# Folding a pooling mixer's product into the output weights, and a re-ordered start of the kernel

## The chip, the cores and the metric

The kernel runs on one core of a Trainium2 chip. The metric is the device time of one execution in microseconds (us), lower is better. The engines are TensorE (PE in the profile, its weight loads PEld), VectorE (DVE), ScalarE (ACT), GpSimd (POOL) and SyncE (SP), which issues nearly all transfers between DRAM and on-chip memory.

## The reference

One transformer-like layer (DEPTH = 1) is computed in fp32 for a prompt of 2048 tokens and a sample of 64, D = 1024, four heads of 128, feed-forward width 2816:

```
mod = c_act @ w_ada + b_ada                        # adaLN shifts, scales, gates
h   = rmsnorm(x) * g1 * (1 + scale1) + shift1
u, q, k, v, o, gates = split(h @ w_in)
diff = pooled(u) - u                               # 4 groups of 128, windows 2, 4, 8, 16
y    = einsum('btgc,gcd->btgd', diff, w_pool) * s_pool
x   += gate1 * (concat(y, mlstm(q, k, v, o, gates)) @ w_out)
x   += gate2 * (conv_gated(norm(x) @ w_up) @ w_down)
out  = rmsnorm(x) * g_final
```

The pooling mixer's y is thus a linear function of `diff`: for group gi, y @ w_out[rows of gi] is diff @ (w_pool[gi] * s_pool) @ w_out[rows of gi].

## The kernel before

**Arithmetic.** Each fp32 operand of a large product is split into two fp32r halves, hi (a rounded copy) and lo (the remainder), and a product is three fp32r matmuls (hi hi, hi lo, lo hi). A weight block is split by `work_out`: ScalarE writes hi (L345), VectorE writes lo (L348). Small steps (row sums with ones, transposes, gate columns, the heads' 128 x 128 products) are plain fp32; such a matmul leaves two records in the profile.

**Stages.** Four groups of tokens (512, 512, 512, 576) go through the attention part one after the other: v's projection (`proj_v`, L1018; for group 0 `first`, L949), four heads (`proj_qko`, with `gemm` L411, and `lstm`, whose fp32 steps are L1158 to L1246), four pooling inputs (`gemm`) each followed by `poolmix` (L1302), then `outproj` (`gemm`, L574 adds the residual). Three groups of 704 tokens go through the feed-forward part (L1444 and L1698), which the change leaves alone.

**The pooling product.** `poolmix` forms diff, splits it, multiplies it by the split w_pool (`WPO`, three matmuls at L1302 for each block of tokens), and writes the scaled result as two halves again (ScalarE L1304, VectorE L1305), which `outproj` multiplies by w_out's rows.

**Weights.** `issue` starts the load of the next block of the list `stream`; `pump` keeps up to seven split blocks (WB) and four raw ones (RB) on the way. In group 0 a block's split halves are stored in DRAM (`hl_kept`, by `keep`, L353), and groups 1 to 3 load these (512 KB, for v 528 KB) instead of a raw block (256 or 264 KB).

**The start.** `first` loads x, then the adaLN weights for shift1 and scale1 in four quarters (`load_q`, `mod_q`: products L864, transpose L870), and for each quarter makes two of h's eight row blocks (`h0`: L888, L889, L893) and their v products (`cells`). It needs the reciprocal norms in every partition, which TensorE makes by ones (`pr`, L929).

**Order.** The start up to v's projection of group 0 is in hand-written order. In the rest of the attention part a scheduler orders each engine's instructions by its own estimates; the program gives it side work in generators that are ticked at set places: bg[3] is `ada` (the rest of the adaLN modulation: VectorE steps L180 and L182 on streamed w_ada, then sums by ones L190 and transposes L197), others are `rstd_rows` (reciprocal norms, L466 and L473), the next group's norm, the lstm heads. Every engine runs its instructions in order, SyncE its transfers too.

Of the kernel before, what the change touches and what calls it, by code (L numbers as in the profile page):

```python
# [16 lines left out]
P = 128  # L17
# [20 lines left out]
WB, RB = 7, 4  # L38
# [7 lines left out]
NV = 360  # L46

C_ID = 0

C_L127, C_L63, C_CNT = 0, 128, 256  # L50
NCST = 448
# [3 lines left out]
def tile_layer(ctx: ExitStack, tc: tile.TileContext, xT, vecs, cst, rst, rowv, w_mod, w_ada, w_qkou, w_v, w_pool,  # L55
# [51 lines left out]

    live = [0]
# [5 lines left out]
    x0 = [big(mx.tile([P, 2, TMAX], F32R, tag="mx", name=f"mx{k}")) for k in range(KD)]  # L114
    for k in range(KD):
        (act if k % 2 else nc.sync).dma_start(out=x0[k][:, :GT], in_=xT[k, :, 0:GT])
    V = cp.tile([P, NV], F32, tag="V", name="V")
    nc.sync.dma_start(out=V, in_=vecs)
    ident = cp.tile([P, P], F32, tag="ident", name="ident")
    nc.sync.dma_start(out=ident, in_=cst[:, C_ID:C_ID + P])  # L120
    RV = cp.tile([4, 3], F32, tag="RV", name="RV")
    nc.sync.dma_start(out=RV, in_=rowv)
# [26 lines left out]
    def ada(m, first):  # L149
# [36 lines left out]
        yield  # L186
# [6 lines left out]
        yield  # L193
# [11 lines left out]
        yield  # L205
# [29 lines left out]
    U_ORDER = (3, 2, 1, 0)  # L235
    OUT, INSIDE, WHOLE = range(3)
    stream = []

    hl_kept = dr.tile([40, P, 2, WN], F32, tag="hl_kept", name="hl_kept")
# [12 lines left out]
    for g in range(NG):  # L252
        rows = [[halves((hv, kh), w_v[hv][kh], 4 * VC[hv]) for kh in (0, 1)] for hv in (1, 0)]
# [9 lines left out]
        for n in range(KD):  # L263
            stream += [(w_out[n][:, c:c + 512], 512) for c in (512, 0)]
# [196 lines left out]
    def rstd_rows(ssum, o, out):  # L461
# [8 lines left out]
        yield  # L470
# [73 lines left out]
    def stat2(o, ssum):  # L544
        for _ in range(5):
            yield
        out = RS2[:, 4 * o.g:4 * o.g + len(o.chunks)]
        if o.last:
            rstd_cols([ssum], o, out)
        else:  # L550
            yield from rstd_rows(ssum, o, out)
        yield

    def outproj(o, mix, between):
# [28 lines left out]
        bg[0].append(stat2(o, ssum))  # L583
# [193 lines left out]
    if True:  # L777
# [3 lines left out]
        C = a1.tile([P, NCST - P], F32, tag="C", name="C")  # L781
# [31 lines left out]

        def rows_of(o):
# [9 lines left out]
        def norm1(o, xs, box):  # L824
# [8 lines left out]
            yield from rstd_rows(ssum, o, rs)  # L833
            yield
# [7 lines left out]
        spare_rows = [x[:, GT:2 * GT] for x in x0]  # L842
        c_q = [spare_rows,
# [5 lines left out]
        def load_q(qn):  # L849
            for k in range(KD):  # L850
                tc.keep_in_program_order(nc.sync.dma_start(out=c_q[qn][k], in_=w_mod[qn, k]))
# [996 lines left out]
```

## Time and profile before

| what | value |
|---|---|
| median of 3 runs | 2243.78 us (2242.88 to 2245.01) |
| profiled execution | 2241.11 us, its span 2239.3 us |
| TensorE busy | 2215.4 us (99%) |
| VectorE / ScalarE busy | 1568.4 us (70%) / 990.7 us (44%) |
| first product of a head (L411) | at 58.91 us |
| mean granted TensorE clock | 0.995 |
| moved by DMA | 493.71 MB, mean 220 GB/s |

The span runs from the first to the last instruction of the profiled execution. The clock is TensorE's granted one, 1.00 is full speed. A group of instructions has a busy time and a mean duration; since matmuls overlap in the array, the mean of one is longer than the step from one to the next in an unbroken run. "Idle before" is the time that an engine stood still ahead of an instruction, with what ended it. A timeline gives an instruction's start, its duration, and in brackets the idle time ahead of it; a run of equal instructions is one row. The DMA share is the mean busy share of 16 DMA engines.

### The profile page before, as it was taken

Reading aid. Unit: us, or ns where it says so; the run is one execution under the profiler, and the core shown is the slowest. Engines: PE = TensorE matmul, PEld = TensorE weight load, DVE = VectorE, ACT = ScalarE, POOL = GpSimd, SP = SyncE. Lnnn points to the kernel's source line nnn. Section 1 sums busy time; section 2 is a strip of 40 time slices with the busy share of each in tenths; the row PEclk is TensorE's granted clock in tenths of the full one; section 3 lists DMA queues with packets and bytes.
Section 4 is the critical chain, followed back from the end, with each engine's and each line's share of the span. In section 5 each row is a group of like instructions: output and inputs, shape, how many; then the busy total and the mean of one; then the engine's idle time right before and its main releaser. Section 6 shows DMA issues by size and latency. Waiting matters only on the chain. (4 is left out here: it accounts for less than half of the span.)

```text
span 2239.3 us, 37881 instructions
## 1 busy us (share of the span) xinstructions
PE 2215.4 (99%) x13720; PEld 2100.6 (94%) x13720; DVE 1568.4 (70%) x2878; ACT 990.7 (44%) x1968; POOL 209.1 (9%) x482
## 2 busy tenths in 40 slices
PE   8999999999999999999999999999999999999998
PEld 6888888888899999999999999999999999999997
DVE  4878558667855788687858587777666675767474
ACT  3544335234233455465536344545444343435254
POOL 0010000001000230010000210100001210101012
PEclk8999999999999999999999999999999999999999
DMA  9967997997989485657556884566448655353442
GB/s 337 337 244 257 336 300 224 331 314 234 308 286 308 131 268 174 224 174 261 196 177 229 267 272 159 173 202 199 144 160 287 199 170 163 116 172 111 149 144 79
DMA packets 286139, 493.71 MB, mean 220 GB/s; under 512 B 24920, under 2 KB 88920, under 8 KB 285952
## 3 DMA queue, kind: packets, MB, share of 16 engines
q1 hardware_dynamic: 276480, 468.97, 63.5%
q10 hardware_dynamic: 9472, 22.32, 2.6%
q8 instruction: 108, 1.77, 0.3%
q14 instruction: 79, 0.65, 0.1%
HBM read 382.97 MB, written 108.22 MB: 219 GB/s over the span
## 5 line engine op out<-in xcount | busy, mean ns | idle before, releaser
L1444 PE MATMUL mm<-hx,wt 128*128 128x352 f32 x5544 | 898.4, 323 | 2.8 <-DVE wt L348 2.0
L1444 PEld LDWEIGHTS mm<-hx,wt 128*128 128x128 f32 x5544 | 893.1, 188 | 3.7 <-DVE wt L348 2.3
L1698 PE MATMUL mm<-av,wt 128*128 128x352 f32 (+2 forms) x3168 | 514.4, 323 | 0.0
L1698 PEld LDWEIGHTS mm<-av,wt 128*128 128x128 f32 x3168 | 509.0, 188 | 1.6
L411 PE MATMUL mm<-hl,wt 128*128 128x512 f32 (+2 forms) x1920 | 390.6, 358 | 1.2 <-DVE wt L348 0.9
L411 PEld LDWEIGHTS mm<-hl,wt 128*128 128x128 f32 x1920 | 314.2, 188 | 53.2 <-issue 5.3
L348 DVE TENSOR_TENSOR wt<-raw,wt 128x512 fp32r<-128x512 f32 (+3 forms) x494 | 307.1, 637 | 71.3 <-ACT wt L345 68.3
L345 ACT ACTIVATE wt<-raw 128x512 fp32r<-128x512 f32 (+3 forms) x494 | 270.6, 570 | 158.6 <-PE mm L1698 71.1
L1714 DVE SCALAR_TENSOR_TENSOR x<-mm,MOD,x 128x352 f32<-128x352 f32 (+4 forms) x224 | 106.4, 525 | 126.1 <-PE mm L1698 126.0
L411 PE MATMUL mm<-mx,wt 128*128 128x512 f32 (+1 forms) x960 | 187.6, 355 | 0.3 <-DVE scr L574 0.2
L411 PEld LDWEIGHTS mm<-mx,wt 128*128 128x128 f32 x960 | 159.1, 188 | 26.8 <-ACT mx L1304 1.0
L1431 DVE SCALAR_TENSOR_TENSOR tg<-eg,V,tg 128x704 f32<-128x704 f32 (+1 forms) x132 | 125.7, 952 | 53.8 <-ACT tg L1426 51.5
L348 DVE TENSOR_TENSOR wt<-wt 128x512 fp32r<-128x512 f32 x176 | 122.1, 694 | 37.2 <-ACT wt L345 37.0
L1431 DVE SCALAR_TENSOR_TENSOR ta<-ea,V,ta 128x704 f32<-128x704 f32 (+1 forms) x132 | 125.6, 952 | 5.3 <-ACT ta L1426 2.6
L345 ACT ACTIVATE wt<-wt 128x512 fp32r<-128x512 f32 x176 | 108.5, 623 | 25.2 <-DMA wt<-wsum 20.9
L1492 ACT ACTIVATE u<-mm 128x352 f32<-128x352 f32 x66 | 30.6, 464 | 165.4 <-PE mm L1444 161.2
L1452 DVE TENSOR_TENSOR eg<-mm,u 128x352 f32<-128x352 f32 x154 | 70.2, 468 | 42.0 <-ACT u L1507 28.3
L1552 DVE TENSOR_TENSOR av<-tg,av 128x704 fp32r<-128x704 f32 (+1 forms) x88 | 60.5, 708 | 53.1 <-ACT av L1547 53.0
L1538 ACT ACTIVATE tg<-tg 128x704 f32<-128x704 f32 (+1 forms) x66 | 52.4, 794 | 78.7 <-DVE tg L1431 78.7
L1483 ACT ACTIVATE s<-mm 128x352 f32<-128x352 f32 x66 | 30.5, 462 | 102.4 <-PE mm L1444 100.2
L1018 PE MATMUL mm<-wt,hl 128*128 128x256 f32 (+1 forms) x576 | 72.4, 285 | 0.0
L1018 PEld LDWEIGHTS mm<-wt,hl 128*128 128x128 f32 x576 | 70.7, 188 | 1.0 <-issue 0.6
(295 smaller groups left out, 1993.5 us busy)
## 6 DMA issues: line engine op xcount, KB each, us to landing
wt<-hl_kept SPq DMA_DIRECT2D x108, 512.0 KB, 5.8
raw<-w_up SPq DMA_DIRECT2D x198, 256.0 KB, 4.0
wt<-wsum SPq DMA_DIRECT2D x176, 256.0 KB, 4.4
wt<-wsplit SPq DMA_DIRECT2D x88, 512.0 KB, 5.0
raw<-w_down SPq DMA_DIRECT2D x96, 256.0 KB, 3.8
w<-w_up SPq DMA_DIRECT2D x88, 256.0 KB, 4.2
wsum<-w SPq DMA_DIRECT2D x44, 512.0 KB, 4.7
wsplit<-wt SPq DMA_DIRECT2D x44, 512.0 KB, 4.5
```

Of the source, the lines that this page charges most:

```text
L345: act.activation(u.w[:, 0, :u.n], u.raw[:, :u.n], AF.Copy)
L348: dve.tensor_tensor(out=u.w[:, 1, :u.n], in0=u.raw[:, :u.n], in1=u.w[:, 0, :u.n].bitcast(F32), op=ALU.subtract)
L411: pe.matmul(ps[bi][:, :hi - lo], U[:, a, k % 4 * P:(k % 4 + 1) * P], mv[k][:, b, lo:hi], start=(at == 0 and pi == 0), stop=(k == order[-1] ...
L1018: pe.matmul(ps[ti][:n, :cols], h[4 * kh + k4][:, b, lo:lo + n], U[:, a, k4 % 2 * cols:(k4 % 2 + 1) * cols], start=(kh == 0 and k4 == 0 and ...
L1431: dve.scalar_tensor_tensor(out=t[:, :E], in0=ext[:, j:j + E], scalar=wc(j, f), in1=t[:, :E], op0=ALU.mult, op1=ALU.add)
L1444: pe.matmul(ps[:, :FH], U[:, a, kc * P:(kc + 1) * P], Bo.at(nm, kc, b), start=(first and kc == 0 and pi == 0), stop=(kc == 3 and pi == 2), ...
L1452: dve.tensor_tensor(out=ext[:, d:d + b - a], in0=ps[:, a:b], in1=u[:, a:b], op=ALU.add)
L1492: act.activation(self.u2, b1[:, :FH], AF.Copy)
L1538: act.activation(self.tg[:, :E], self.tg[:, :E], AF.Silu)
L1552: dve.tensor_tensor(out=self.d[:, 1, a:b], in0=self.tg[:, a + 2 * s:b + 2 * s], in1=self.d[:, 0, a:b].bitcast(F32), op=ALU.subtract)
L1698: pe.matmul(ps[i][:, :hi - lo], U[:, a, k % 4 * P:(k % 4 + 1) * P], av[k][:, b, lo:hi], start=(k == 0 and (a, b) == PASSES[0]), stop=(k == ...
L1714: dve.scalar_tensor_tensor(out=x3[n][:, a:b], in0=ps[i][:, a - lo:b - lo], scalar=gt2(n, s), in1=x3[n][:, a:b], op0=ALU.mult, op1=ALU.add)
```

## The change

Five things are changed at once.

1. *Fold.* A new generator `fold` multiplies w_out's first 512 columns of each of the eight blocks (all that touches the pooled rows) once by w_pool scaled by s_pool (`WPT`, the transposed w_pool, scaled on ScalarE): 32 plain-fp32 matmuls (L843 of the changed kernel) in eight steps, eight ScalarE copies, four loads and four stores of 512 KB; `outproj` streams the result `wo_in` in place of these columns. `poolmix` ends with the split of diff: L1302, L1304 and L1305 are gone. w_out's pieces are loaded into buffers (`w4`, four of them) that `ada` uses as well.
2. *Queue of fp32 steps.* `fold`, the end of `ada` (`ada_end`) and `rstd_rows` are put into a list `side`; `extra()` runs one step of it, at three places of the gates' work and three of each head, next to fp32 steps that stand there already.
3. *First loads.* x comes in four loads of 512 KB, three of the four adaLN quarters in pairs; the identity and the gate biases lie in `vecs`, without loads of their own.
4. *Start.* `pr` comes after five of the eight blocks of the first adaLN quarter; x is multiplied by `pr` straight from PSUM; two matmuls whose result is not used stand ahead of v's products; of the first quarter the products with hi rows come first; a quarter's adaLN products are one block behind 6, 4 or 4 runs of three v products (PRE), no longer mixed with these.
5. *v.* The split halves of v's weights are not stored; groups 1 to 3 load the raw blocks and split them again (eight blocks a group). RB is 5.

In the order of the built kernel TensorE's start reads as follows (before: L864 adaLN products, L929 `pr`, L870 transpose, L949 v's products; the tile names behind `<-` are the operands). Before:

```order
L864 MATMUL m_183<-mx_90,CA 2x128 x4
L864 MATMUL m_183<-mx_91,CA 2x128 x4
L929 MATMUL pr<-scr,ones_r 128x512
L870 MATMUL m_184<-ident,scr 128x128
L949 MATMUL mm<-wt,hl_306 128x264 x12
L949 MATMUL mm<-wt,hl_307 128x264 x3
L864 MATMUL m_183<-q,CA 2x128 x8
L864 MATMUL m_183<-k,CA 2x128 x8
L949 MATMUL mm<-wt,hl_307 128x264 x3
L864 MATMUL m_183<-th,CA 2x128 x8
L949 MATMUL mm<-wt,hl_307 128x264 x3
L864 MATMUL m_183<-at,CA 2x128 x8
```

With the change (L905 is now the adaLN product, L983 `pr`, L914 the transpose, L996 the unused products, L1014 v's):

```order
L905 MATMUL m_168<-mx_90,CA 2x128 x4
L983 MATMUL pr<-scr,ones_r 128x512
L905 MATMUL m_168<-mx_90,CA 2x128 x4
L905 MATMUL m_168<-mx_91,CA 2x128 x8
L914 MATMUL m_169<-V,scr 128x128
L996 MATMUL pr<-mx_87 128x256 x2
L1014 MATMUL mm<-wt,hl_291 128x264 x8
L1014 MATMUL mm<-wt,hl_292 128x264 x8
L1014 MATMUL mm<-wt,hl_291 128x264 x2
L905 MATMUL m_168<-q,CA 2x128 x8
L905 MATMUL m_168<-k,CA 2x128 x8
L905 MATMUL m_168<-th,CA 2x128 x8
```

`pr` moved ahead of the last 12 adaLN products, and the next quarter's products stand together.

TensorE in group 0's first head, from the transpose of the gates' rows (L1110 before) to the products with the transposed gates `CL` (L1122) and the first 128 x 128 product of keys and queries. Before:

```order
L1110 MATMUL m_911<-ident,R_188 128x128 x4
L411 MATMUL mm<-hl_594,wt 128x512 x3
L411 MATMUL mm<-hl_306,wt 128x512 x3
L411 MATMUL mm<-hl_307,wt 128x512 x3
L1170 MATMUL m_956<-ident,k 128x128 x4
L411 MATMUL mm<-hl_393,wt 128x512 x3
L411 MATMUL mm<-hl_394,wt 128x512
L1122 MATMUL m_929<-CL,C 128x16
L1158 MATMUL m_949<-RHL,E_r 128x512
```

With the change (L1170 is now that transpose, L429 the heads' product, L1183 the product with CL, L843 the fold):

```order
L1170 MATMUL m_892<-V,R_173 128x128 x4
L843 MATMUL m_901<-w_751,WPT 128x128 x4
L429 MATMUL mm<-hl_567,wt 128x512 x3
L1183 MATMUL m_916<-CL,C 128x16
L843 MATMUL m_919<-w_751,WPT 128x128 x4
L429 MATMUL mm<-hl_291,wt 128x512 x3
L429 MATMUL mm<-hl_292,wt 128x512 x3
L1220 MATMUL m_945<-RHL,E_r 128x512
L1232 MATMUL m_952<-V,k 128x128 x4
L1242 MATMUL m_958<-q,k 128x128 x4
L843 MATMUL m_964<-w_926,WPT 128x128 x4
```

Between the transpose and the product with CL stood thirteen matmuls of the heads' product and a transpose of k; now a fold step and three matmuls stand there.

VectorE around v's projection of group 1 (L574 is outproj's residual, L182 an adaLN step on streamed w_ada, L1032 the gates' copy after a v product, L803 a sum of w_up's blocks). Before:

```order
L574 SCALAR_TENSOR_TENSOR scr<-mm,MOD,scr 128x512
L446 TENSOR_TENSOR ssum<-ssum,scr 128x512
L180 TENSOR_SCALAR s_2678<-raw,CA 128x512
L180 TENSOR_SCALAR acc<-raw,CA 128x512
L182 SCALAR_TENSOR_TENSOR s_2678<-raw,CA,s_2678 128x512
L182 SCALAR_TENSOR_TENSOR acc<-raw,CA,acc 128x512
L1032 COPY gt<-mm 128x8
L803 TENSOR_TENSOR w_2312<-w_2312 128x256
```

With the change (L589, L198, L1091 and L821 are these; L366 is the split's lo half):

```order
L589 SCALAR_TENSOR_TENSOR scr<-mm,MOD,scr 128x512
L198 SCALAR_TENSOR_TENSOR s_2541<-raw,CA,s_2541 128x512
L198 SCALAR_TENSOR_TENSOR u<-raw,CA,u 128x512
L464 TENSOR_TENSOR ssum<-ssum,scr 128x512
L198 SCALAR_TENSOR_TENSOR s_2541<-raw,CA,s_2541 128x512
L198 SCALAR_TENSOR_TENSOR u<-raw,CA,u 128x512
L198 SCALAR_TENSOR_TENSOR s_2541<-raw,CA,s_2541 128x512
L366 TENSOR_TENSOR wt<-raw,wt 128x512
L1091 COPY gt<-mm 128x8 x3
L198 SCALAR_TENSOR_TENSOR u<-raw,CA,u 128x512
L1091 COPY gt<-mm 128x8
L366 TENSOR_TENSOR wt<-raw,wt 128x512
```

Two splits of v's blocks now stand among the adaLN steps.

The diff, cut to its core:

```diff
-WB, RB = 7, 4
+WB, RB = 7, 5
+FIRST, PRE = 5, (6, 4, 4)
+    side = []
+    def extra():
+        while side:
+            try:
+                next(side[0])
+                return
+            except StopIteration:
+                side.pop(0)
...
     for g in range(NG):
-        rows = [[halves((hv, kh), w_v[hv][kh], 4 * VC[hv]) for kh in (0, 1)] for hv in (1, 0)]
+        rows = [[[(w_v[hv][kh][:, c:c + 2 * VC[hv]], 2 * VC[hv]) for c in (0, 2 * VC[hv])] for kh in (0, 1)] for hv in (1, 0)]
...
-            stream += [(w_out[n][:, c:c + 512], 512) for c in (512, 0)]
+            stream += [(w_out[n][:, 512:], 512), (wo_in[n], 512)]
...
+        def fold():
+            for n in range(0, KD, 2):
+                w = a1.tile([P, 4, 256], F32, tag="w4", name="w4", bufs=4).rearrange("p (a b) c -> p a (b c)", a=2)
+                nc.sync.dma_start(out=w, in_=w_out[n:n + 2, :, :512].rearrange("n p c -> p n c"))
+                yield
+                for i in range(2):
+                    t = w[:, i]
+                    ps = m2_ps()
+                    for gi in range(4):
+                        c = slice(gi * P, (gi + 1) * P)
+                        pe.matmul(ps[:, c], WPT[:, c], t[:, c], start=True, stop=True)
+                    act.activation(t, ps, AF.Copy)
+                    if i == 0:
+                        yield
+                nc.sync.dma_start(out=wo_in[n:n + 2].rearrange("n p c -> p n c"), in_=w)
...
             mod = mod_q(0)
-            for _ in range(KD):
+            for _ in range(FIRST):
                 next(mod)
-            load_q(3)
...
             pe.matmul(pr, ones, dg[:, :GT], start=True, stop=True)
             act.activation(pb[0], pr, AF.Copy)
+            for k in (0, 1):
+                dve.tensor_tensor(out=x0[k], in0=x0[k], in1=pr, op=ALU.mult)
+            for _ in range(KD - FIRST):
+                next(mod)
+            load_q(3)
...
+            for _ in range(2):
+                pe.matmul(pr[:, :256], x0[7][:, :P], x0[7][:, :256], start=True, stop=True)
...
                 if qn < 3:
-                    for _ in range(5):
+                    for _ in range(PRE[qn]):
                         next(row)
                     mod = mod_q(qn + 1)
                     for i in range(KD):
                         next(mod)
-                        if i in (3, 5):
-                            next(row)
                     next(mod)
                     next(row)
-                    next(row)
                     for _ in mod:
                         pass
                     us = h0(2 * qn + 2)
...
-                        for v in used:
-                            keep(v)
...
             split(mix, df[:, :o.T], o.T)
             yield
-            sc = V[:, V_SP + gi:V_SP + gi + 1]
-            for (lo, hi) in o.blks:
-                pp = m2_ps()
-                for (pi, (wi, di)) in enumerate(((0, 0), (1, 0), (0, 1))):
-                    pe.matmul(pp[:, :hi - lo], WPO[:, wi, gi * P:(gi + 1) * P], mix[:, di, lo:hi],
-                              start=(pi == 0), stop=(pi == 2))
-                act.activation(mix[:, 0, lo:hi], pp[:, :hi - lo], AF.Copy, scale=sc)
-                dve.scalar_tensor_tensor(out=mix[:, 1, lo:hi], in0=pp[:, :hi - lo], scalar=sc,
-                                         in1=mix[:, 0, lo:hi].bitcast(F32), op0=ALU.mult, op1=ALU.subtract)
-            yield
```

More of the change, by code (lines that the diff above doesn't have):

```diff
@@ L544, in stat2 @@
     def stat2(o, ssum):
+        out = RS2[:, 4 * o.g:4 * o.g + len(o.chunks)]
         for _ in range(5):
             yield
[L547 to L551, printed above, removed]
+        rstd_cols([ssum], o, out)
         yield
@@ L582, in outproj @@
                 sq_acc(ssum, x[:, :o.T], o.T, n == 0)
-        bg[0].append(stat2(o, ssum))
+        if o.last:
+            bg[0].append(stat2(o, ssum))
+        else:
+            side.append(rstd_rows(ssum, o, RS2[:, 4 * o.g:4 * o.g + len(o.chunks)], []))
     fgroups = []
@@ L832, in norm1 @@
             rs = sm.tile([P, 5], F32, tag="rs", name="rs")
-            yield from rstd_rows(ssum, o, rs)
-            yield
+            done = []
+            side.append(rstd_rows(ssum, o, rs, done))
+            while not done:
+                yield
             yield
@@ L846, in tile_layer @@
                [t[:, i * 512:(i + 1) * 512] for t in [big(hl_tile(k)) for k in range(4)] for i in range(2)],
-               spare_rows]
+               c0]
         def load_q(qn):
-            for k in range(KD):
-                tc.keep_in_program_order(nc.sync.dma_start(out=c_q[qn][k], in_=w_mod[qn, k]))
-            for _ in range(2):
-                issue()
+            pin = tc.keep_in_program_order
+            for k in range(0, KD, 2):
+                if qn == 1:
+                    for i in (k, k + 1):
+                        pin(nc.sync.dma_start(out=c_q[qn][i], in_=w_mod[qn, i]))
+                else:
+                    pin(nc.sync.dma_start(out=pair_of(c_q[qn][k:k + 2]), in_=w_mod[qn, k:k + 2].rearrange("k p t -> p k t")))
+                if k >= 4:
+                    issue()
         for qn in range(3):
@@ L885, in h0 @@
             work_out(us[0], 1)
-            xs = [(k, x0[k][:, :GT], hl_tile(k)) for k in (k0, k0 + 1)]
+            xs = [(k, x0[k], hl_tile(k)) for k in (k0, k0 + 1)]
+            if k0 == 0:
+                for k, x, d in xs:
+                    act.activation(d[:, 0, :GT], x, AF.Identity, scale=G1[:, k, 0:1], bias=sh1(k, 0))
+                    h.append(d)
+                work_out(us[0])
+                for k, x, d in xs:
+                    dve.tensor_scalar(out=x, in0=x, scalar1=G1[:, k, 0:1], scalar2=sh1(k, 0), op0=ALU.mult, op1=ALU.add)
+                    dve.tensor_tensor(out=d[:, 1, :GT], in0=x, in1=d[:, 0, :GT].bitcast(F32), op=ALU.subtract)
+                work_out(us[1])
+                return us
             for k, x, d in xs:
@@ L906, in first @@
             for k in range(KD):
[L907 removed]
+                x, sq = x0[k], scr()
                 act.activation(sq[:, :GT], x, AF.Square)
@@ L1023, in part @@
                         tick(0)
-                    if ti % 2 == 0:
+                    if hv == 0 and ti % 2 == 0:
                         tick(3)
@@ L1347, in tile_layer @@
                 nc.sync.dma_start(out=t[:, :512], in_=w_pool.rearrange("p g c -> p (g c)"))
-                split(WPO, t[:, :512], 512)
+                for gi in range(4):
+                    act.activation(WPT[:, gi * P:(gi + 1) * P], t[:, gi * P:(gi + 1) * P], AF.Copy,
+                                   scale=V[:, V_SP + gi:V_SP + gi + 1])
+                side.append(fold())
             if o.g == 0:
@@ L1367, in tile_layer @@
             drain(3)
+            while side:
+                extra()
             quiet.append(1)
```

90 lines of the change are left out of this document (49 added, 41 removed).

## The prediction

> **What bounds the kernel now.** I read the page's engine line first, then TensorE's waits, the span cut into stages, and last the timelines of the stages that the change touches.
>
> ```profile
> span 2239.3 us, 37881 instructions
> PE 2215.4 (99%) x13720; PEld 2100.6 (94%) x13720; DVE 1568.4 (70%) x2878; ACT 990.7 (44%) x1968; POOL 209.1 (9%) x482
> ```
>
> TensorE is busy for 2215.4 of 2239.3 us, so an edit gains what it takes out of TensorE's own work, or out of its waits. These are few (columns: who waited for whom, us in total, times, longest):
>
> ```profile
> PE m L917 <- DMA mx<-xT: 4.8, 1, 4.8
> PE mm L949 <- DVE hl L893: 2.2, 4, 0.6
> PE mm L949 <- ACT hl L889: 2.1, 1, 2.1
> PE mm L1444 <- DVE wt L348: 2.0, 1, 2.0
> PE mm L411 <- DVE wt L348: 0.9, 1, 0.9
> ```
>
> The two L949 rows, 4.3 us, are in group 0's v stage, which the change rewrites. By stage (columns: stretch, its length, busy time of PE, PEld, DVE, ACT, POOL, granted clock, DMA share, GB/s):
>
> ```profile
> 4.77:14.60 9.83, 8.78 (x72) 6.62 (x72) 4.13 (x10) 4.48 (x9) 1.10 (x2) 1.00 0.99 344
> 14.60:21.30 6.70, 4.33 (x36) 1.09 (x28) 2.92 (x8) 1.94 (x4) 0.00 (x0) 0.50 1.04 394
> 21.30:28.30 7.00, 6.40 (x50) 5.05 (x50) 3.33 (x6) 1.73 (x3) 0.00 (x0) 0.51 1.04 386
> 28.30:58.90 30.60, 29.01 (x339) 25.35 (x339) 17.05 (x39) 10.60 (x21) 0.00 (x0) 1.00 0.93 330
> 60.00:100.00 40.00, 39.13 (x193) 31.87 (x193) 34.40 (x64) 22.34 (x49) 1.19 (x1) 1.00 1.00 356
> 220.00:250.00 30.00, 30.00 (x234) 28.47 (x233) 16.85 (x33) 8.48 (x16) 1.01 (x1) 1.00 1.00 336
> ```
>
> Two facts matter: for some 14 us near the start TensorE had half its clock, and from 60 to 100 us, where the fold will run, VectorE is 86% busy and the transfers are at their limit. The v stage of group 1 (220 to 250) leaves VectorE 13 us and ScalarE 21 us free.
>
> **The pool product.** Its matmuls, and rows that give a price for one:
>
> ```profile
> L1302 PE MATMUL m<-mx,WPO 128*128 128x512 f32 x36 | 10.3, 394 | 0.0
> L1302 PE MATMUL m<-mx,WPO 128*128 128x320 f32 x12 | 2.4, 311 | 0.0
> L1302 PE MATMUL m<-mx,WPO 128*128 128x256 f32 x12 | 2.1, 282 | 0.0
> 30.97 2.78 PE L949 MATMUL p<-wt,hl 128*128 128x256 f32 x21
> 61.08 7.64 PE L411 MATMUL mm<-hl,wt 128*128 128x512 f32 x32
> 83.41 1.05 PE L1194 MATMUL m<-va,kw 128*128 128x129 f32 x8
> ```
>
> The 276 to 400 ns of single matmuls overlap, so I take the pace of unbroken runs: the last one's 0.4 us off, 7.64 us is (7.64 - 0.40)/31 = 0.234 us for 512 columns, and (2.78 - 0.28)/20 = 0.125 us for 256. For 320 I interpolate to 0.152. Removed: 36 x 0.234 + 12 x 0.125 + 12 x 0.152 = 11.7 us.
>
> The fold adds 32 plain-fp32 matmuls of 128 columns. A plain-fp32 matmul leaves two records; the L1194 run gives (1.05 - 0.28)/7 = 0.11 us for a record, so 64 x 0.11 = 7.1 us. The upper bound is a record's share when such spells are counted with their edges, 1.05/8 = 0.13, hence 8.4 us. Net: **-4.6 us**, between -3.3 and -4.6. All of it is on the path, because TensorE does not wait in the heads or in the pool stage. Twenty ScalarE and twenty VectorE evacuations go too, off the path; eight ScalarE copies come.
>
> **Queuing fp32 steps.** By the order of the built kernel, the plain-fp32 spells between the heads' first and the FFN's first product go from 92 to 81. What does one cost beyond its matmuls?
>
> ```profile
> 69.59 7.49 PE L411 MATMUL mm<-hl,wt 128*128 128x512 f32 x31 [0.87 <-DVE wt L348]
> 76.92 0.60 PE L1110 MATMUL m<-ident,R 128*128 128x128 f32 x4
> 77.27 2.34 PE L411 MATMUL mm<-hl,wt 128*128 128x512 f32 x9
> 80.82 0.29 PE L1122 MATMUL m<-CL,C 128*128 128x16 f32 x2
> ```
>
> The L1110 spell holds the next product up from 76.92 to 77.27, 0.35 us for four records that are worth 0.44 at 0.11: nothing is lost by the change of kind. In the start's cycles (below) a return to three v products after a spell costs 0.18. So 11 x (0 to 0.18) = 0 to -2 us; I take **-0.5**, nearer to the heads' own row.
>
> **The start.** Group 0's v stage runs in cycles: products of a quarter of the rows, adaLN products of the next quarter, a transpose, the next quarter's normalized rows (h) on ScalarE and VectorE.
>
> ```profile
> 16.91 2.08 PE L929 MATMUL pr<-scr,ones_r 128*128 128x512 f32 x2
> 21.26 0.59 PE L949 MATMUL mm<-wt,hl 128*128 128x264 f32 x1 [2.06 <-ACT hl L889]
> 22.45 3.45 PE L949 MATMUL mm<-wt,hl 128*128 128x264 f32 x14 [0.60 <-DVE hl L893]
> 30.94 0.27 PE L870 MATMUL m<-ident,scr 128*128 128x128 f32 x1
> 33.59 0.28 PE L949 MATMUL mm<-wt,hl 128*128 128x264 f32 x1
> 34.40 1.95 PE L949 MATMUL mm<-wt,hl 128*128 128x264 f32 x14 [0.53 <-DVE hl L893]
> 37.27 0.63 PE L949 MATMUL mm<-wt,hl 128*128 128x264 f32 x3
> 37.83 0.62 PE L864 MATMUL m<-hl,CA 128*2 128x128 f32 x16
> 43.76 1.95 PE L949 MATMUL mm<-wt,hl 128*128 128x264 f32 x14 [0.53 <-DVE hl L893]
> 58.91 1.32 PE L411 MATMUL mm<-hl,wt 128*128 128x512 f32 x5
> ```
>
> (a) Begin. v's products run unbroken from 22.45. In the change `pr` (2.08 us) no longer waits for all adaLN products, but three eighths of them now follow it, and the transpose, two small VectorE steps and h still follow those: I get a first product at 21 to 22, with the hi halves first so that it need not pause for the lo half. Gain 0.5 us, 0 to 1.5.
>
> (b) Cycles. A cycle lasts 43.76 - 34.40 = 9.36 us. Twice in it three v products stand between two adaLN spells; such a visit takes 37.83 - 37.27 = 0.56 us where three at 0.128 make 0.38, so 0.18 is lost each time, some 0.5 a cycle with the third visit. That falls away as the adaLN products become one block. Each cycle also ends in a stall: 3.46 us lie between the transpose at 30.94 and the second product at 34.40, and TensorE had 2.65 us of work for them (30.94 to 33.59). The change has three more runs of three products behind the transpose (nine, 1.15 us), 3.8 to 4.2 us of cover against 3.46, so the stall and the pause around it (0.53, 0.65 with the lone first product) should go. Three cycles x 1.15 = 3.5 us.
>
> (c) The half clock. It ended at 28.3, 5.9 us after products ran unbroken from 22.45; half a microsecond earlier start, and two dummy matmuls, bring that forward by about as much, worth half of it in time: 0.25 to 0.5.
>
> Sum: **-4.5 us**. Bounds: 0, if the transfers (share 1.04 until 28.3) set the pace, and -9, if the clock does not fall at all.
>
> **Group 0's first head.** The change puts the step that needs the transposed gates (CL) nearer to its source: by the order, TensorE has three products and eight fold records after the transpose, 0.70 + 0.89 = 1.6 us, where the rows above show 3.6 us (77.27 to 80.82).
>
> ```profile
> 78.90 0.73 DVE L182 SCALAR_TENSOR_TENSOR s<-w,CA,s 128x512 f32<-128x512 f32 x1
> 79.56 0.15 DVE L1114 COPY CL<-m 128x16 f32<-128x16 f32 x1
> w<-w_ada SPq DMA_DIRECT2D x16, 256.0 KB, 6.6
> ```
>
> VectorE copies CL at 79.56, behind its adaLN steps (0.73 each). TensorE would be there at 77.27 + 1.6 = 78.9, so it waits about 0.8 us. The next fold step needs rows loaded into a buffer that an adaLN step has to free, and such a load lands 6.6 us after its issue: another 0 to 4 us. Against it the 0.87 us stall before 69.59 may go. I take **+1**, 0 to +5.
>
> **v's split weights.** Groups 1 to 3 no longer load 528 KB of split halves but raw ones, and split them again: eight units a group, 24 in all.
>
> ```profile
> L348 DVE TENSOR_TENSOR wt<-raw,wt 128x512 fp32r<-128x512 f32 (+3 forms) x494 | 307.1, 637 | 71.3 <-ACT wt L345 68.3
> L345 ACT ACTIVATE wt<-raw 128x512 fp32r<-128x512 f32 (+3 forms) x494 | 270.6, 570 | 158.6 <-PE mm L1698 71.1
> hl_kept<-wt SPq DMA_DIRECT2D x4, 528.0 KB, 6.0
> 255.87 0.75 DVE L182 SCALAR_TENSOR_TENSOR s<-raw,CA,s 128x512 f32<-128x512 f32 x1 [3.06 <-DMA raw<-w_ada]
> ```
>
> Per group that is 8 x 0.57 = 4.6 us on ScalarE and 8 x 0.64 = 5.1 us on VectorE, in a stage of 24 us in which they have more than that free. A unit feeds 24 products, 3 us, against 1.3 us for its two halves, so the splits keep ahead: **+0.25**, 0 to +0.5 while the work covers them. Without that cover each unit would cost 1.3 us, 31 in all. Eight stores (4.2 MB) and half of each load leave the queues; the fold's four loads and four stores (4.2 MB) come, in a stretch where the share is 1.00.
>
> **Sum.** -4.6 - 0.5 - 4.5 + 1 + 0.25 = -8.4 us. The profiled execution took 2241.1 us (span 2239.3 and 1.8 around it): 2232.7 after. The median of the three timed runs is 2243.8, 2.7 above the profiled one; on that scale **2235.4**.
>
> **Rivals.**
>
> 1. *The clock does not fall.* In the 13.7 us at half speed TensorE was busy for 4.33 + 6.40 = 10.7, which would take half as long. New work in the gap, and the earlier v products, might keep the clock up: some 4.5 us more, 2231. Against it: the loads still set when the first 20 us can begin, and the fall at 14.6 came although TensorE had been busy for 8.78 of the 9.83 us before. Chance 0.14. [...]
>
> 2. *Transfers bind the start.* The DMA share is 1.04 up to 28.3. If the quarters' rows arrive no earlier, the stalls move to the adaLN products and the 4.5 us stay: -3.9, 2240. Against it: from 28.3 to 58.9 the share is 0.93, and TensorE's only waits there are for VectorE. Chance 0.15.
>
> 3. *The fold stalls the heads.* Buffers shared with adaLN steps, a VectorE at 86% and transfers at 1.00: TensorE, in order, stands before a fold step at +5 in place of +1: 2239.5. Chance 0.11.
>
> 4. *Slower: v's splits queue behind adaLN steps.* VectorE runs in order, and in the new order two of a group's splits stand between L182's steps, which wait for loads (3.06 us at 255.87; before, no product hung on such a wait). If a wait of 3 us stands ahead of both, and the split has less than a unit's 3 us of lead, each costs its 3 us: 3 x 2 x 3.06 = 18 us, -8.4 + 18 = +10, 2254 (with half of the six late 2245). It decides once the raw loads of v run less than about 3 us ahead. Chance 0.10.
>
> **Numbers.** Forecast 0.50, own range 2232 to 2239. A change of 0.2%, 4.5 us, is what a measurement here can tell; 2239.3 is the line. Below it lie the forecast, rival 1 and somewhat under half of rivals 2 and 3: 0.49 + 0.14 + 0.10 = 0.73. Of rival 4 nine tenths lie above 2248.3: 0.09; the rest, 0.18, within. The range takes in rivals 1 to 3: 2228 to 2242.
>
> **What would show it.** Right: no L1302, 64 fold records at 0.11 us a step; the first head product near 54.5 instead of 58.91; no L949-type stall for VectorE; TensorE's v stages of groups 1 to 3 unbroken. Wrong: a granted clock of 1.00 from 14 to 28; adaLN products waiting for w_mod; TensorE idle in front of a fold step between 70 and 90; v products waiting for VectorE's split.

## The result

The changed kernel takes 2231.22 us (median of 4 runs, 2228.88 to 2231.92) beside 2243.33 for the kernel before (4 runs, 2238.78 to 2245.01): a ratio of 0.995, 95% interval 0.9938 to 0.9962. Timed once more in the last experiment it took 2229.72 us (6 runs) beside 2242.01 (17 runs), 0.9945, interval 0.9932 to 0.9959. So it is some 12 us faster by the medians (12.1 and 12.3); 8.4 were forecast. The profiled executions differ by less, 2241.1 and 2231.9 us, 9.2.

The head of the changed kernel's page, and TensorE's five longest waits with a shorter one (columns as before):

```profile
span 2230.1 us, 37946 instructions
PE 2206.6 (99%) x13728; PEld 2097.5 (94%) x13728; DVE 1571.7 (70%) x2882; ACT 1002.1 (45%) x1984; POOL 214.4 (10%) x482
```

```profile
PE m L972 <- DMA mx<-xT: 5.9, 2, 5.6
PE m L1686 <- DVE fscr L1679: 2.2, 1, 2.2
PE mm L1504 <- DVE wt L366: 1.6, 1, 1.6
PE m L1114 <- ACT va L1092: 1.3, 2, 1.0
PE m L1183 <- ACT CL L1176: 1.1, 1, 1.1
PE m L1077 <- DVE scr L1118: 0.6, 1, 0.6
```

TensorE still sets the end. The waits for h at the start (4.3 us) are gone; small new ones have come: 1.1 us for CL and 1.3 for the gates (L1114: 0.3 in group 0's first head, 1.0 in the last group's v stage). The 2.2 us at L1686, at the end of the feed-forward part, are in the kernel before as well. By stretches (length, PE, PEld, DVE, ACT, POOL, clock, DMA share, GB/s):

```profile
4.77:15.50 10.73, 8.79 (x72) 6.84 (x72) 4.13 (x9) 4.48 (x9) 0.93 (x1) 1.00 1.05 390
15.50:22.30 6.80, 5.53 (x32) 2.78 (x32) 3.24 (x8) 2.50 (x5) 0.17 (x2) 0.50 1.05 388
22.30:52.30 30.00, 30.00 (x389) 28.47 (x389) 21.09 (x47) 13.45 (x27) 0.00 (x0) 1.00 1.01 370
54.00:100.00 46.00, 44.74 (x236) 36.91 (x236) 39.59 (x72) 26.21 (x57) 2.06 (x1) 1.00 0.91 328
220.00:244.00 24.00, 24.00 (x206) 23.19 (x205) 15.72 (x30) 7.14 (x13) 0.00 (x0) 1.00 0.96 332
```

The half clock between 10 and 35 us lasted 6.8 us in place of 13.7, and from 22.3 to 52.3 TensorE did not pause. Group 1's v stage, with eight splits more, has no pause either. TensorE's timeline through the start and the first head (start, duration, work, idle before):

```profile
22.07 2.61 PE L1014 MATMUL mm<-wt,hl 128*128 128x264 f32 x18
26.96 0.33 PE L914 MATMUL m<-V,scr 128*128 128x128 f32 x1
30.32 1.74 PE L1014 MATMUL mm<-wt,hl 128*128 128x264 f32 x12
31.99 1.93 PE L905 MATMUL m<-hl,CA 128*2 128x128 f32 x64
38.49 1.61 PE L1014 MATMUL mm<-wt,hl 128*128 128x264 f32 x12
52.28 1.54 PE L429 MATMUL mm<-hl,wt 128*128 128x512 f32 x6
70.03 1.06 PE L843 MATMUL m<-w,WPT 128*128 128x128 f32 x8
70.85 0.94 PE L429 MATMUL mm<-hl,wt 128*128 128x512 f32 x3
72.87 0.40 PE L1183 MATMUL m<-CL,C 128*128 128x16 f32 x2 [1.08 <-ACT CL L1176]
77.58 1.13 PE L843 MATMUL m<-w,WPT 128*128 128x128 f32 x8
174.87 44.64 PE L429 MATMUL mm<-mx,wt 128*128 128x512 f32 x192
219.35 14.66 PE L1077 MATMUL mm<-wt,hl 128*128 128x264 f32 x120
```

The same places of the kernel before, where group 0's outproj and group 1's v stage begin:

```profile
174.92 4.33 PE L411 MATMUL mm<-mx,wt 128*128 128x512 f32 x18
221.00 8.93 PE L1018 MATMUL mm<-wt,hl 128*128 128x264 f32 x72
```

The time can be followed through these starts. The first head begins 6.6 us earlier (58.91, 52.28). Group 0's heads take 122.6 us in place of 116.0, since the fold is in them, so that outproj begins at the same time (174.92, 174.87). Outproj is 1.6 us shorter (46.1, 44.5), without two of the group's pool products. From there the later groups and the feed-forward part bring the rest of the 9.2 us, in steps of 0 to 2.5 us; one step goes the other way, the last group's v stage, which takes 32.4 us in place of 30.8.

### The profile page after: what moved, and what is told of

Its sections match the earlier page's. It is cut to its first block, busy times and chain, and to the rows that moved or that the text cites. A ratio compares the mean times of both kernels' runs of the same rounds, so it can differ in the third digit from the quotient of the medians.

```text
span 2230.1 us, 37946 instructions
## 1 busy us (share of the span) xinstructions
PE 2206.6 (99%) x13728; PEld 2097.5 (94%) x13728; DVE 1571.7 (70%) x2882; ACT 1002.1 (45%) x1984; POOL 214.4 (10%) x482
## 4 chain that ended last, share of the span: by engine, by line
PE 89%; DMA 5%; DVE 3%; issue 1%; SPq 0%; ACT 0%; POOL 0%; POOLq 0%; DVEq 0%; ACTq 0%
PE mm L1504 40%; PE mm L1758 23%; PE mm L429 20%; PE mm L1077 2%; DMA hl_kept<-wt 1%; DMA wsum<-w 1%; DMA raw<-w_v 1%; DMA raw<-w_ada 1%; DMA mx<-xT 1%; PE m L1257 1%; PE m L1277 1%; PE m L1279 1%; PE m L1242 1%; DVE hx L728 1%; PE m L1232 0%
## 5 line engine op out<-in xcount | busy, mean ns | idle before, releaser
L429 PE MATMUL mm<-hl,wt 128*128 128x512 f32 (+2 forms) x1920 | 388.7, 358 | 0.0
L363 ACT ACTIVATE wt<-raw 128x512 fp32r<-128x512 f32 (+3 forms) x518 | 286.3, 574 | 215.8 <-PE mm L429 81.6
L366 DVE TENSOR_TENSOR wt<-raw,wt 128x512 fp32r<-128x512 f32 (+3 forms) x518 | 323.2, 640 | 84.5 <-ACT wt L363 79.3
L429 PEld LDWEIGHTS mm<-hl,wt 128*128 128x128 f32 x1920 | 314.6, 188 | 52.2 <-issue 5.3
L429 PE MATMUL mm<-mx,wt 128*128 128x512 f32 (+1 forms) x960 | 185.3, 354 | 0.0
L429 PEld LDWEIGHTS mm<-mx,wt 128*128 128x128 f32 x960 | 159.1, 188 | 25.4
L366 DVE TENSOR_TENSOR wt<-wt 128x512 fp32r<-128x512 f32 x176 | 121.9, 694 | 34.0 <-ACT wt L363 33.0
```

What stands on the lines that cost most here:

```text
L363: act.activation(u.w[:, 0, :u.n], u.raw[:, :u.n], AF.Copy)
L366: dve.tensor_tensor(out=u.w[:, 1, :u.n], in0=u.raw[:, :u.n], in1=u.w[:, 0, :u.n].bitcast(F32), op=ALU.subtract)
L429: pe.matmul(ps[bi][:, :hi - lo], U[:, a, k % 4 * P:(k % 4 + 1) * P], mv[k][:, b, lo:hi], start=(at == 0 and pi == 0), stop=(k == order[-1] ...
```

## The experiments

The kernels fall into three sets: one part of the change taken out (e1 to e4, e7), one part or two put into the kernel before (e5, e6, e9, e10), and repeats or additions (e8, e11, e12). None has the new first loads apart from the new order. The code cuts show the core of an edit; three dots stand for what is left out. Times are medians, ratios are against the kernel before on the same chip.

### e1_nofold: the pooling product as before

```diff
-                side.append(fold())
+                split(WPO, t[:, :512], 512)
...
-            stream += [(w_out[n][:, 512:], 512), (wo_in[n], 512)]
+            stream += [(w_out[n][:, c:c + 512], 512) for c in (512, 0)]
...
+                    pe.matmul(pp[:, :hi - lo], WPO[:, wi, gi * P:(gi + 1) * P], mix[:, di, lo:hi],
+                              start=(pi == 0), stop=(pi == 2))
```

> The changed kernel with the pooling product as before (three matmuls per block in each group, w_out's columns streamed as they are), everything else as changed. Theory (the fold is worth its matmuls): group 0's stretch from the first head product to outproj gets shorter by the 7 us of fold records and the 1.1 us wait for CL, less 1.4 us for two pool products; every group's pool and outproj together longer by 2.8, 2.8, 2.8 and 3.3 us; in all +3.5 to +4.6, 2235 to 2236. Rival (the fold's spells delay group 0's heads by more than their own records): less than +2, 2233 or below.

Measured: 2240.31 us (10 runs), 0.9988 of the kernel before, interval 0.9977 to 0.9999. The fold's removal costs 9.1 us, twice the 4.6 of its matmuls. In the profiled executions (2239.4 against 2230.1) the difference lies in three places: group 0's heads are only 3.3 us shorter (119.3, 122.6), not 6.7; the four outprojs are longer by 1.5, 1.6, 1.3 and 2.1; heads and feed-forward part of the later groups bring the rest. In group 0 two longer waits eat a part of what the missing fold saves:

```profile
54.30 0.27 PE L1114 MATMUL m<-V,gt 128*4 128x128 f32 x1 [0.79 <-ACT va L1092]
73.03 0.40 PE L1183 MATMUL m<-CL,C 128*128 128x16 f32 x2 [1.75 <-ACT CL L1176]
```

In the changed kernel these were 0.33 and 1.08 us: the fold step ahead of L1183 takes up a part of a wait that is there without it. Another part is the clock, which in this execution fell twice more, in group 0's heads and early in the feed-forward part (columns as in the stretches above):

```profile
74.41:77.83 3.42, 3.42 (x14) 2.67 (x13) 2.18 (x4) 2.27 (x7) 0.00 (x0) 0.50 1.06 401
815.11:818.52 3.41, 3.41 (x13) 3.41 (x12) 2.56 (x5) 2.18 (x4) 1.58 (x1) 0.50 0.92 330
```

TensorE was busy throughout both, so each is worth up to 1.7 us (an estimate: half of 3.4). The profiled execution of the changed kernel has neither, and so some 3 of these 9.3 us are not the fold's. Neither theory's time was hit.

### e2_keepv: v's split halves stored and loaded again

```diff
-        rows = [[[(w_v[hv][kh][:, c:c + 2 * VC[hv]], 2 * VC[hv]) for c in (0, 2 * VC[hv])] for kh in (0, 1)] for hv in (1, 0)]
+        rows = [[halves((hv, kh), w_v[hv][kh], 4 * VC[hv]) for kh in (0, 1)] for hv in (1, 0)]
...
+                        for v in used:
+                            keep(v)
```

> The changed kernel, but v's split halves are stored by group 0 and loaded by groups 1 to 3, as before. Theory (24 more splits fill VectorE's and ScalarE's queues in the v stages, and so TensorE waited 1.0 and 0.6 us in the last group's v stage): that stage falls from 32.4 to 30.8 us, v stages of groups 1 and 2 stay at 24.4 to 24.6, 2229.5 in all. Rival (these waits come from the adaLN steps, which wait for their loads ahead of the gates' copy wherever v's halves come from): the stage stays at 32 us or the wait moves to another place, 2231 to 2233.

Measured: 2231.43 us (4 runs), 0.9949. The last group's v stage fell from 32.4 to 31.0 us, as the theory had it, but nothing was won: TensorE waited elsewhere, 1.0 us for each of two things in group 0's heads. And the repeat of the changed kernel (e12) has that stage at 31.3 us, so the 32.4 was in good part one execution's. Its wait can be read on VectorE of the changed kernel:

```profile
602.82 0.75 DVE L198 SCALAR_TENSOR_TENSOR s<-raw,CA,s 128x512 f32<-128x512 f32 x1 [1.60 <-DMA raw<-w_ada]
603.49 0.42 DVE L822 TENSOR_TENSOR w<-w 128x256 f32<-128x256 f32 x1
603.83 0.15 DVE L1091 COPY gt<-m 64x8 f32<-64x8 f32 x1
```

An adaLN step waits 1.60 us for its load, and the copy of the last gates stands behind it; TensorE then waited 1.02 us for these. It is the mechanism of the fourth rival, in small, on the gates and not on v's splits.

### e3_noside: adaLN ends and reciprocal norms at their own places

```diff
-        side.append(ada_end(m, accs))
+        yield from ada_end(m, accs)
...
-            side.append(rstd_rows(ssum, o, rs, done))
-            while not done:
-                yield
+            yield from rstd_rows(ssum, o, rs, [])
```

> The changed kernel, but the ends of the adaLN steps and the reciprocal norms are issued at their own places again; only the fold is queued. TensorE's plain-fp32 spells between the first head and the feed-forward part go from 81 back to 93. Theory (a spell costs nothing beyond its matmuls): within 0.6 us, 2231 to 2232. Rival (a change of kind costs 0.18 us each way seen at the start): +2.2 us, 2233.4.

Measured: 2233.05 us (4 runs, 2229.91 to 2234.71), 0.9953, interval 0.9936 to 0.9971, with 93 spells against 81. The runs spread too far to tell 0.6 from 2.2 us. The profiled execution is 2.1 us shorter than the changed kernel's (2228.0, 2230.1), of which 1.4 are its start (no half clock). No cost of twelve more spells is seen.

### e4_mixed: adaLN products mixed with v's again

```diff
-FIRST, PRE = 5, (6, 4, 4)
+FIRST, PRE = 5, (5, 5, 5)
...
                     for i in range(KD):
                         next(mod)
+                        if i in (3, 5):
+                            next(row)
                     next(mod)
                     next(row)
+                    next(row)
```

> The changed kernel, but the adaLN products of quarters 2 to 4 stand mixed with v's products in the order of the kernel before (five runs ahead, one after blocks 4 and 6, two behind the transpose). Theory (the block order saves the three changes of kind and the stall for h's lo half): a cycle of the start goes from 8.0 back to 9.2 us or so, first head product at 55.5 to 56, 2234.5. Rival (what shortened the start is the clock's earlier return alone): first head product at 52.3 to 53, 2231 to 2232.

Measured: 2235.03 us (5 runs), 0.9961. The start of this execution, with the same 6.8 us of half clock as the changed kernel's:

```profile
22.08 2.09 PE L1014 MATMUL mm<-wt,hl 128*128 128x264 f32 x15
31.61 1.97 PE L1014 MATMUL mm<-wt,hl 128*128 128x264 f32 x14 [0.56 <-DVE hl L948]
40.98 1.96 PE L1014 MATMUL mm<-wt,hl 128*128 128x264 f32 x14 [0.53 <-DVE hl L948]
50.35 3.06 PE L1014 MATMUL mm<-wt,hl 128*128 128x264 f32 x23 [0.59 <-DVE hl L948]
56.13 1.09 PE L429 MATMUL mm<-hl,wt 128*128 128x512 f32 x4
```

The stalls for h's lo half are back, a cycle takes 40.98 - 31.61 = 9.37 us where the changed kernel has 38.49 - 30.32 = 8.17, and the first head begins at 56.13 instead of 52.28: 3.85 us, and 3.8 by the medians (5.3 against the changed kernel's in e12). The theory holds; the rival falls.

### e5_foldonly: the fold alone in the kernel before

```diff
+        def fold():
...
-            stream += [(w_out[n][:, c:c + 512], 512) for c in (512, 0)]
+            stream += [(w_out[n][:, 512:], 512), (wo_in[n], 512)]
...
-                split(WPO, t[:, :512], 512)
+                side.append(fold())
```

> The kernel before with the fold alone (its queue holds nothing else; start, loads, v's stored halves, RB of 4 as before). Theory A (pool products are worth 11.7 us, the fold 6.6 of records, and a little for waits): 4 to 5 us faster than the kernel before, 2237 to 2238.5. Theory B (the fold is worth the 9 us that taking it out of the changed kernel cost, because the pool products also held up ScalarE and VectorE): 2233 to 2234. In both: group 0's stretch from the first head product to outproj 121 to 123 us (116.0 before), each outproj 1.4 to 2.1 us shorter.

Measured: 2239.48 us (10 runs) beside 2242.63, 0.9988, interval 0.9978 to 0.9998: 3.2 us faster. Group 0's heads take 123.3 us and the outprojs of groups 0 to 2 44.5 or 44.6. That is theory A's mechanism, at a little less than its price.

### e6_before_dummy, e7_nodummy: the two unused matmuls

The first adds these two lines to the kernel before, ahead of the first v product; the second takes them out of the changed kernel.

```diff
+            for _ in range(2):
+                pe.matmul(pr[:, :256], x0[7][:, :P], x0[7][:, :256], start=True, stop=True)
```

> The kernel before with the two unused matmuls between the transpose of the first adaLN quarter and the first v product, nothing else. Theory (TensorE's pause of 2.1 us ahead of v's products is what kept the clock at half until 28.3): half clock ends at 19 to 23 us, first head product at 56 to 57 in place of 58.9, 2 to 3 us faster, 2240. Rival (the half clock's length is chance, or the pause doesn't matter): the half clock still ends at 25 to 29 in this execution, 2242 as before.

> The changed kernel without the two unused matmuls. Theory (they keep TensorE busy and bring the full clock back): half clock to 25 us or later, first v products 1 to 2 us slower, first head product at 53 to 55 in place of 50.9 to 52.3, 2233. Rival (TensorE's pause there is short enough without them): half clock as in the changed kernel (0 to 6.8 us long), 2231.

Measured: the kernel before with them 2238.32 us (9 runs), 0.9979, interval 0.9965 to 0.9993, so 4.3 us faster, more than the 2 to 3 of the theory; the changed kernel without them 2232.21 us (4 runs, 2229.86 to 2236.62), 1 to 2.5 us slower than with them, inside the spread. In the profiled execution of the first the clock read 1.00 from 10 to 35 us, and the first head began at 54.54. In that of the second the half clock lasted 10.2 us and reached into v's products, which took 4.09 us where the changed kernel's first 18 took 2.61:

```profile
22.16 4.09 PE L1012 MATMUL mm<-wt,hl 128*128 128x264 f32 x18 [1.37 <-ACT hl L934]
```

Both times go the theory's way; but the half clock's length changes from one execution of a kernel to the next (e8, e12), so these two profiles do not prove it. The mean granted clocks of all their runs point the same way, 0.9972 with the two matmuls in the kernel before against 0.9961 without, 0.9960 without them in the changed kernel against 0.9972 and 0.9980 with them; e9, which has them, is at 0.9962 and goes against it.

### e8_before_again: the kernel before, a second profile

The kernel is unchanged.

> The kernel before once more, for a second profile of its start. If the half clock of 13.7 us is its rule: 13 to 14 us again, first head product at 58.9. [...]

Measured: one run, 2243.09 us. From 10 to 35 us of the span, the kernel before, first in the execution of the first profile, then in this one (the clock is the third number from the end):

```profile
10.00:35.00 25.00, 20.55 (x204) 14.12 (x203) 11.97 (x28) 6.69 (x12) 1.10 (x2) 0.73 1.02 375
```

```profile
10.00:35.00 25.00, 19.92 (x246) 14.62 (x244) 12.54 (x28) 6.75 (x12) 1.10 (x2) 0.93 1.03 379
```

The mean clock was 0.73 and 0.93: 13.7 us and 3.4 us at half. The first head began at 56.75, 2.2 us earlier. So the length is not a property of the kernel: it differs between two executions of the same program. Yet this execution was 2 us longer in all than the first profile's: from the last outproj to the end of TensorE's work it took 3.4 us more (1477.8, 1474.4). About half of that is the clock again, which fell once more there, with TensorE busy throughout; in the first profile it stayed at 1.00 in this stretch:

```profile
814.40:817.82 3.42, 3.42 (x14) 3.42 (x13) 2.22 (x7) 1.72 (x4) 1.51 (x1) 0.50 0.80 279
```

### e9_startonly, e10_foldstart: new start alone, and with the fold

The changed kernel with the pool product as in e1, v as in e2, fp32 steps as in e3 and RB = 4 is e9; the same with the fold left in is e10. Of their edits only the last is shown here.

```diff
-WB, RB = 7, 5
+WB, RB = 7, 4
```

> The new start and first loads alone: pooling product, v's stored halves, the places of the fp32 steps and RB of 4 as before. The fold alone gave -3.2 us and everything but the fold -2.0, which does not add up to the -11 of the changed kernel. Theory A (gains add; v's re-splits or the queue took some away where the fold was left out): -4 to -6, 2237 to 2239. Theory B (an earlier start without the fold is given back: the first head's gate chain on ScalarE and VectorE cannot follow, and TensorE waits for it): first head product at 51 to 53, but outproj of group 0 at 171 to 172 in place of 172.8 to 174.9 (heads 119 us in place of 116), -2, 2240.5.

> The fold and the new start; v's stored halves, the places of the fp32 steps and RB of 4 as before. Theory (v's re-splits and the queued steps are worth nothing either way): as the changed kernel, 2230 to 2232.5, the last group's v stage 30.8 us. Rival (they bring part of the gain, as eight stores fewer leave room for the fold's): 2234 or more.

Measured: e9 takes 2243.14 us (12 runs, 2238.08 to 2244.86), ratio 1.000, interval 0.9991 to 1.0009; e10 takes 2232.83 us (6 runs), 0.9961, interval 0.9947 to 0.9975. The start alone gains nothing in the timed runs, the fold alone 3.2 us, the two together 9.2.

Theory B's place for the loss is wrong: in e9's profiled execution the first head begins at 52.51 and group 0's heads take 116.0 us, as before, so that outproj begins at 168.54, 6.4 us ahead of the kernel before. The lead is still 6.3 us when group 1 ends; by the last outproj 2.4 are left (756.25, 758.64). It goes in the heads of groups 2 and 3 (1.7 and 2.6 us), with waits of TensorE for VectorE's kw, which the kernel before's profile does not have there (kernel e9, two of the waits of the whole span):

```profile
PE m L1262 <- DVE kw L1238: 1.6, 1, 1.6
PE m L1316 <- DVE kw L1238: 1.3, 1, 1.3
```

That explains a part. But this profiled execution, at 2238.08, is the fastest of the twelve, and what a typical one, 5 us longer, loses was not seen. Why the start's gain stays only where the pool products are gone is open. The granted clock accounts for a part: e10's runs have a mean of 0.9970 and the kernel before's beside them 0.9960, which is worth some 2 of the 9.2 us (an estimate, worked out in the last section), while e9 (0.9962) and e5 (0.9961, as the kernel before in its rounds) gained next to nothing in clock. That leaves 7 us for the two together against 0 and 3.2 alone. e10 beside the changed kernel (2232.83 to 2229.7 and 2231.2) leaves 1.6 to 3.1 us for v's re-splits, the queue and the fifth raw buffer together, hardly more than the runs' spread (2231.64 to 2237.64).

### e11_moredummy, e12_after_again: more unused matmuls, and the changed kernel again

```diff
+            for _ in range(1):
+                pe.matmul(ptq[:, :256], x0[7][:, :P], x0[7][:, :256], start=True, stop=True)
             rs = sm.tile([P, 5], F32, tag="rs", name="rs")
             rstd_cols(sums, o0, rs)
...
             for _ in range(FIRST):
                 next(mod)
+            for _ in range(1):
+                pe.matmul(ptq[:, :256], x0[7][:, :P], x0[7][:, :256], start=True, stop=True)
```

> The changed kernel with two more unused matmuls, in TensorE's pauses of 0.7 us ahead of the row sums and 0.9 us ahead of pr. Theory (pauses make the clock fall): clock 1.00 throughout the start in this execution, first v product at 20.8, first head product at 50.9, timed runs 1 us faster and closer together, 2230. [...]

> The changed kernel once more, on the chip of these runs and in the same rounds, for a second profile and a tighter time. If the difference of 11 us holds: 2230 to 2232.5; the sum of its parts would give 2237.

Measured: e11 2230.29 us (6 runs, 2227.62 to 2234.69), e12 2229.72 (6 runs, 2228.65 to 2231.53), no difference. In both profiled executions the clock read 1.00 from 10 to 35 us, so two more matmuls show nothing. The changed kernel without a half clock begins its first head at 50.97:

```profile
20.90 2.48 PE L1014 MATMUL mm<-wt,hl 128*128 128x264 f32 x18
50.97 1.54 PE L429 MATMUL mm<-hl,wt 128*128 128x512 f32 x6
54.09 0.27 PE L1114 MATMUL m<-V,gt 128*4 128x128 f32 x1 [1.58 <-ACT va L1092]
72.81 0.40 PE L1183 MATMUL m<-CL,C 128*128 128x16 f32 x2 [1.02 <-ACT CL L1176]
```

Of the 1.3 us gained over the first profile, 1.25 go at once into a longer wait for the gates (1.58 in place of 0.33), which ends at the same time, 54.1. What stands there can be read on ScalarE of this kernel:

```profile
51.36 0.63 ACT L363 ACTIVATE wt<-raw 128x512 fp32r<-128x512 f32 x1 [0.48 <-DMA raw<-w_qkou]
52.21 1.28 ACT L363 ACTIVATE wt<-raw 128x512 fp32r<-128x512 f32 x2 [0.21 <-DMA raw<-w_qkou]
53.39 1.19 ACT L1092 ACTIVATE va<-p 128x256 f32<-128x256 f32 x4
```

ScalarE's copy of v and the gates (L1092) is queued behind splits of the first head's weights, and those wait for their loads. With v's products done that early, the transfers set when the first head goes on in this execution; a start earlier still would gain nothing there.

## Why the prediction was right, point by point

The measured 2231.2 us lies 4.2 us below the forecast 2235.4, 0.8 below its own range (2232 to 2239) and inside the whole one (2228 to 2242). It is the figure of the first rival (2231). So the direction and the places are right, while the size was hit only in part, and in part for reasons that the sum does not have.

**The bound.** Right: TensorE is busy 99% as before, and its busy time fell from 2215.4 to 2206.6 us, 8.8 of the 9.2 between the two profiles.

**The pool product, -4.6.** The half of the removed matmuls that stood in the outprojs was priced well: these are 1.4 to 1.6 us shorter in the groups of 512 tokens, for two products priced at 1.4. Of the other half, which stood at the end of the heads' stretches, less is seen: these are 0.15, 1.2 and 0.3 us shorter in groups 1 to 3 of the first profile, 1.0, 1.4 and 0.7 in e12. The fold was priced well:

```profile
L843 PE MATMUL m<-w,WPT 128*128 128x128 f32 x64 | 8.6, 277 | 0.0
```

Inside a run its records follow each other by 0.11 us, as forecast. Only the last of each run of eight is followed after 0.03 us by the heads' product, whose second matmul then comes 0.315 behind the first, where 0.234 is usual; both together are again what the two matmuls cost in unbroken runs. As a term of the sum the -4.6 was mis-sized in both directions: the fold alone gained 3.2 us, and taking it out of the changed kernel cost 9.1, of which a part is the clock (e1). The prediction added terms that do not add; it looked for no such link.

**Queuing fp32 steps, -0.5.** Nothing seen of it (e3). Behind the fold's runs nothing is lost by the change of kind (the steps of 0.03 and 0.315 us above), which speaks for a price of 0 in the heads.

**The start, -4.5.** The mechanism was right in (b). Step (a), the begin, brought 0.4 us in the first profile (first v product at 22.07, unbroken, against 22.45; 0.5 forecast). The cycles brought 3.85 us where 3.5 were forecast (e4). Step (c) was too small: 0.25 to 0.5 us were given to an earlier end of the half clock, which took 13.7 us in one profile and 6.8 in the other; that earlier products or the two unused matmuls bring that end forward was the author's estimate, and no run shows it (e6 and e7 do not settle it). At equal half clock the first head is earlier by 4.8 us (3.4 us each: e8 56.75, e1 51.97), by 5.2 (6.8 us each: e5 57.50, the changed kernel 52.28) and by 3.6 (none: e6, which has the unused matmuls, 54.54, e12 50.97). So -4.5 is a fair price of the order for the first head's begin; the other 2 us of the 6.6 were the clock's. As a term of the sum it is not borne out: the start alone gained 0 in the timed runs (e9), and beside the fold some 6 (9.2 less 3.2). The prediction also read the clock's row of 4.77 to 14.60 as 1.00 throughout, where TensorE ran at half speed up to some 7.7 us (0.427 us from record to record, 0.216 from 8.6 on; last section).

**Group 0's first head, +1.** Right in the place: 1.08 us in front of the product with CL, 0.8 forecast. VectorE's copy of CL stands behind an adaLN step, as thought, and ScalarE's part of CL behind that copy (changed kernel):

```profile
71.77 0.75 DVE L198 SCALAR_TENSOR_TENSOR u<-w,CA,u 128x512 f32<-128x512 f32 x1
72.43 0.17 DVE L1174 COPY CL<-m 128x16 f32<-128x16 f32 x1
72.63 0.34 ACT L1176 ACTIVATE CL<-m 128x16 f32<-128x16 f32 x3 [1.96 <-DVE CL L1174]
```

The wait for the fold's second load did not come: the step at 77.58 follows the one before it without a wait that the trace shows. The stall before 69.59 went as thought, and a wait of 0.33 to 1.58 us for the gates came, which was not foreseen.

**v's split weights, +0.25.** Right: storing them again makes 0.2 to 1.7 us of difference to the changed kernel's two medians, within the spread (e2), and group 1's v stage has no pause.

**The sum.** By the profiled executions 9.2 us against 8.4. By the medians it is 12: the profiled execution of before was one of the faster ones (2241.1; the medians in four sets of runs are 2242.0 to 2243.3), which the scale of the forecast allowed for with the same 2.7 us on both sides, while the changed kernel's runs lie around or below its profiled one (2231.9). That the sum comes near the 9.2 is in part luck: no run shows its two large terms, -4.6 and -4.5, as gains that add.

**The rivals.** The first, whose sign was a clock of 1.00 from 14 to 28 us, came true, in whole or in part, in some executions: in six of ten profiles with the new start the half clock after 10 us was 3.4 us or less, in four of them none. The second fell for the v stage, since TensorE did not pause from 22.3 to 52.3; right behind it, in front of the first head's gates, transfers do set the pace (e12). The third did not come: no fold step waited (0.0 in the row of L843). The fourth was seen only as a wait of 1.0 us for the gates (e2).

## What to carry to other kernels

Price an algebraic fold by its matmuls at the pace of unbroken runs, but time it with and without the other edits: here the two main edits gained 0 and 3.2 us alone and 9.2 together. Where a stage alternates two kinds of work that feed each other across engines, putting one kind in a block, with enough of the other behind it to cover the chain, gained 1.2 us a cycle. And take more than one profile of a start: its clock differed by 10 us of half speed between two executions of one kernel. Where kernels differ by tenths of a per cent, put each run's mean granted clock beside its time.

## What the runs showed of the hardware

The half clock near the start came in whole pieces. In quarter-microsecond slices of 14 profiled executions, its total between 10 and 35 us is 0 (five), 3.41 (three), 6.83 (four), 10.24 (one) or 13.65 us (one): 0 to 4 times 3.41. It began between 14.5 and 22.5 us, with TensorE busy in 8.79 of the 10.73 us before it (the changed kernel's first stretch). In e5 it came in two separate pieces, 15.1 to 18.5 and 21.9 to 25.3. The longest pause of TensorE between 10 and 30 us in any of the 14 is 2.12 us, in e5 and e8. What makes the clock fall is not shown.

In the first profiles of both kernels TensorE also begins at half speed. The clock's records in these two traces start only at 7.71 us (before) and 8.67 (with the change), and a stretch before them reads 1.00, but the matmuls show it. Both kernels begin with eight products of x's blocks with themselves whose result is not used (L917 before, L972 with the change), two records each. In the changed kernel the first eight of these records take 3.51 us, and the other eight, all behind the clock's first record, take 1.99:

```profile
5.57 3.51 PE L972 MATMUL m<-mx 128*128 128x256 f32 x8 [5.57 <-DMA mx<-xT]
9.37 1.99 PE L972 MATMUL m<-mx 128*128 128x256 f32 x8 [0.29 <-DMA mx<-xT]
```

From one record to the next it is mostly 0.427 us in the first run and 0.216 in the second. In the kernel before it is mostly 0.427 us up to 7.5 us and 0.216 from 8.6 us on.

Later in the span the rows above show single pieces of 3.4 us at half clock in e1 (from 74.4 and from 815.1 us) and e8 (from 814.4). What set these off is open.

The kernel's medians do not follow the start alone: executions of one kernel on one chip spread by 6 to 11 us (2236.71 to 2247.81 in 18 runs of before, 2238.35 to 2248.24 in 17), more than the at most 4.4 us by which the first head's begin varies with the old start in these profiles (58.91 and 54.54), and the new kernel's by 3. Much of this spread goes with the mean granted clock of a run, which was recorded for each: of those 17 runs the six at 0.997 or 0.998 took 2238.35 to 2241.38 us, the three at 0.994 took 2246.16 to 2248.24. As TensorE is busy 99% of the span, 0.001 of clock should be worth some 2.2 us (an estimate: 0.001 of 2240), and these groups lie about 7 us apart for 0.003 to 0.004. In the start, where TensorE pauses, it is worth less: 10.2 us more of half clock, 5.1 us of clock lost, moved the first head by 2.2 (e8). The changed kernel's six runs of e12 have a mean of 0.9980, the 17 beside them 0.9960. By this estimate some 4 of the 12 us go with the clock, and about 8 are left for work and waits; how much of the higher clock the change itself brings is not shown.
